# A decoder layer's output projection by Strassen's seven block products, in three phases with shared weight blocks

## The chip, the cores and the metric

The kernel runs on one core of one Trainium2 chip. The metric is the device time of one execution in microseconds (us), as the median of several runs; lower is better.

## What is computed

One layer of a decoder with an attention mixer, on 512 tokens of width 4096, in float32:

```
x: (1, 512, 4096)   64 query heads of 64, 8 key/value heads, window 128
h    = rms_norm(x, norm_g)
q, k, v, z = split(h @ w_in + b_in)          # w_in: 4096 x 9216
o    = banded attention with sinks (q, k, v) # (512, 4096)
x    = x + (o * silu(z)) @ w_out + b_out     # w_out: 4096 x 4096
out  = rms_norm(x, final_g)
```

The change is in the last two lines: the product with `w_out` and what follows it.

## The kernel before

All matmuls keep float32 accuracy by splitting each operand into a rounded part ("hi", float32r) and the rest ("lo"): ScalarE (ACT) casts hi (L143), VectorE (DVE) subtracts lo = source - hi (L144), and TensorE (PE) forms hi*hi + hi*lo + lo*hi, three matmuls of 128 columns of weights by 512 moving columns. All matmuls are issued by the helper `mm` (L112) and keep the order of the program on PE; on the other engines and queues a scheduler sets the order when the kernel is built.

The program has three stages. First V is projected and x is split (32 steps). Then 68 tiles of the input projection follow, each 8 chunks of 12 matmuls, with attention woven between the chunks (`at`, `tick`); `finish` (L510, L511) multiplies a head pair's output by its gate and writes it to a buffer `gT` in DRAM, from the POOL queue. During the last of these tiles `load_g` (L138) brings the gated outputs g back to SBUF, 512 tokens wide.

The third stage is the output projection, a loop over eight blocks of 512 output columns (`cc`), each over 32 K-tiles (`kt`) and four token blocks (`tb`):

```
for kt in kts:                               # mm_out
    if kt % 2 == 0: raw = load_w(w_out[cc, kt // 2])   # 512 KB on the SP queue, L170
    split_g(kt)                              # g split again for each cc
    w = split_w(raw, kt % 2)
    for tb, acc in enumerate(accs): mm_block(acc, tb, kt, *w)   # 3 matmuls each
```

That is 8 x 32 x 4 x 3 = 3072 matmuls. `bring` (L698 to L705) loads bias, gain and residual on POOL's queue and adds them on POOL, `land` (L711 to L714) adds the PSUM result and squares it, and after the last column block `scale_out` (L668 to L692) forms the norm and stores the rows. In the last column block the final ten K-tiles are held in SBUF (`held`), so that the token blocks end one after another. Tiles of x, g and their splits live in the pool `xg`, weights in `wpool`, attention's tiles in `att`, whose memory is free when attention has ended; the output's tiles (`outp`) are put there.

## Time and profile before

| | us |
|---|---|
| median of 3 runs (2407.26 to 2407.3) | 2407.3 |
| the profiled execution: its own time | 2406.92 |
| the profiled execution: span from first to last instruction | 2405.2 |
| output projection on PE, first to last matmul | 696.4 |
| PE busy, share of the span | 99% |
| DVE / ACT / POOL busy | 58% / 41% / 14% |

The sums of the prediction are made against the profiled execution, whose own time is 1.7 us over its span and 0.4 us under the median. An idle time on an engine that is not waited for costs nothing, so the question at each place is which wait ends last there. A granted clock of 1.00 is 2.4 GHz on TensorE, 0.50 is 1.2 GHz.

### The profile page before, as it was taken

To read this page: it belongs to the slowest core of one execution; us is meant where nothing else is said; L and a number is where in the kernel's file an instruction comes from. 1 tells how busy PE (TensorE), PEld (TensorE's weight loads), DVE (VectorE), ACT (ScalarE), POOL (GpSimd) and SP (SyncE) were. 2 spreads that over 40 slices of the span, in tenths; PEclk is the share of its full clock that TensorE was granted. 3 is DMA by queue.
4 is the path that set the end of the run, shared out by engine and by line. 5 is a ranking of instruction groups with operands and counts; after the bars stand their busy time and mean duration, and the time that the engine had idled before them with its cause. 6 is when DMAs were issued, how large, how long until landed. Compare 5 with 4: busy or idle time off the path is not lost.

```text
span 2405.2 us, 30234 instructions
## 1 busy us (share of the span) xinstructions
PE 2392.2 (99%) x10988; PEld 1991.1 (83%) x10988; DVE 1403.9 (58%) x2502; ACT 985.0 (41%) x2129; POOL 340.7 (14%) x472
## 2 busy tenths in 40 slices
PE   9999999999999999999999999999999999999998
PEld 7888888888888888888888888888888888888886
DVE  5446656555575564656656466565764664665565
ACT  6433433434343342433433334334444444444444
POOL 1101111121020121102102011111210110110110
PEclk9999999999999999999999999999999999999999
DMA  9633233233333323333233332334633433333334
GB/s 343 189 93 102 85 110 97 88 112 86 103 99 92 102 89 110 92 94 105 85 105 104 92 99 86 112 97 128 228 123 97 125 123 100 124 124 97 122 119 184
DMA packets 81077, 280.45 MB, mean 117 GB/s; under 512 B 10080, under 2 KB 10080, under 8 KB 80928
## 3 DMA queue, kind: packets, MB, share of 16 engines
q1 hardware_dynamic: 70176, 243.37, 32.7%
q0 software_dynamic: 10608, 34.88, 4.4%
q8 instruction: 86, 1.41, 0.2%
q14 instruction: 63, 0.52, 0.1%
q10 hardware_dynamic: 144, 0.28, 0.0%
HBM read 259.61 MB, written 18.88 MB: 116 GB/s over the span
## 4 chain that ended last, share of the span: by engine, by line
PE 99%; DMA 0%; DVE 0%; POOL 0%; ACT 0%; DVEq 0%; issue 0%; POOLq 0%
PE acc L112 94%; PE ps L112 2%; PE po L112 2%; PE pt L115 1%; DMA xraw<-in_x 0%; POOL wl L425 0%; POOL wh L425 0%; DVE y L688 0%; ACT xhi L241 0%; ACT y L712 0%; DVE xb L711 0%; DVEq L794 0%; DVE y L692 0%; POOL ww L425 0%; DVE y L678 0%
## 5 line engine op out<-in xcount | busy, mean ns | idle before, releaser
L144 DVE TENSOR_TENSOR wlo<-raw,whi 128x512 fp32r<-128x512 f32 x822 | 587.4, 716 | 760.2 <-ACT whi L143 751.5
L143 ACT CAST whi<-raw 128x512 fp32r<-128x512 f32 x821 | 510.7, 622 | 1204.1 <-PE acc L112 1148.3
L112 PE MATMUL acc<-xhi,wlo 128*128 128x512 f32 x2176 | 849.2, 390 | 0.0
L112 PE MATMUL acc<-xhi,whi 128*128 128x512 f32 x2176 | 848.6, 390 | 0.0
L112 PE MATMUL acc<-xlo,whi 128*128 128x512 f32 x2176 | 848.3, 390 | 0.0
L112 PE MATMUL acc<-whi,gs 128*128 128x512 f32 x1968 | 606.0, 389 | 0.0
L112 PEld LDWEIGHTS acc<-xhi,wlo 128*128 128x128 f32 x2176 | 408.4, 188 | 85.8
L112 PEld LDWEIGHTS acc<-xhi,whi 128*128 128x128 f32 x2176 | 409.1, 188 | 81.1
L112 PEld LDWEIGHTS acc<-xlo,whi 128*128 128x128 f32 x2176 | 408.4, 188 | 81.4
L112 PEld LDWEIGHTS acc<-whi,gs 128*128 128x128 f32 x1968 | 369.4, 188 | 76.7
L112 PE MATMUL acc<-wlo,gs 128*128 128x512 f32 x984 | 382.8, 389 | 0.0
L112 PEld LDWEIGHTS acc<-wlo,gs 128*128 128x128 f32 x984 | 184.7, 188 | 38.4
L144 DVE TENSOR_TENSOR gs<-g,gs 128x512 fp32r<-128x512 f32 x256 | 186.8, 770 | 0.7 <-ACT gs L143 0.7
L425 POOL TENSOR_SCALAR_AFFINE_SELECT ww<-wh 64x512 fp32r<-64x512 f32 x64 | 41.7, 651 | 881.7 <-ACT wh L421 881.7
L143 ACT CAST gs<-g 128x512 fp32r<-128x512 f32 x256 | 145.7, 616 | 1.7 <-PE acc L112 1.7
L497 DVE RECIPROCAL e<-e 128x128 f32<-128x128 f32 x128 | 120.6, 944 | 0.5
L399 ACT ACTIVATE prob<-ps,nm 128x128 f32<-128x128 f32 x256 | 90.4, 364 | 74.2 <-DVE nm L390 73.0
L704 POOL DMA_DIRECT2D xb<-in_x x32 | 17.3, 541 | 504.6 <-DVE y L714 430.8
L474 ACT COPY ot<-po 64x256 f32<-64x256 f32 x128 | 46.9, 367 | 56.8 <-DVE o L475 41.2
L475 DVE TENSOR_TENSOR o<-po,ot 64x256 f32<-64x256 f32 x128 | 52.8, 412 | 20.4 <-ACT ot L474 19.8
L348 DVE SCALAR_TENSOR_TENSOR q<-tmp,bcol,q 64x512 fp32r<-64x512 f32 x64 | 58.6, 916 | 7.2 <-ACT q L347 6.2
L274 DVE TENSOR_TENSOR tmp<-acc,rbc 128x512 f32<-128x512 f32 x37 | 25.6, 691 | 57.6 <-PE acc L112 57.6
(125 smaller groups left out, 1629.3 us busy)
## 6 DMA issues: line engine op xcount, KB each, us to landing
raw<-in_w_in SPq DMA_DIRECT2D x272, 512.0 KB, 3.6
raw<-in_w_out SPq DMA_DIRECT2D x128, 512.0 KB, 3.6
row<-in_x POOLq DMA_DIRECT2D x16, 512.0 KB, 6.5
gT<-o POOLq DMA_DIRECT2D x32, 256.0 KB, 2.3
g<-gT SPq DMA_DIRECT2D x16, 512.0 KB, 6.3
xb<-in_x POOLq DMA_DIRECT2D x32, 256.0 KB, 3.6
xraw<-in_xT SPq DMA_DIRECT2D x15, 512.0 KB, 7.1
raw<-in_w_v SPq DMA_DIRECT2D x15, 512.0 KB, 6.4
```

The source lines that it names most:

```text
L112: tc.keep_in_program_order(nc.tensor.matmul(*a, **k))
L115: tc.keep_in_program_order(nc.tensor.transpose(*a, **k))
L143: copy(hi, src),
L144: nc.vector.tensor_tensor(lo, src, hi.bitcast(F32), op=ALU.subtract),
L274: nc.vector.tensor_tensor(t, acc, rbc, op=ALU.mult)
L348: nc.vector.scalar_tensor_tensor(q2[other, :, h, :], tv[own], b[own], q2[own, :, h, :].bitcast(F32), op0=ALU.add, op1=ALU.subtract,)
L399: nc.scalar.activation(pr[:, u, a, :], ps[:, u, a, 0:P], AF.Exp, bias=nm[:, u, a:a + 1], scale=SCALE, accum_out=den[:, u, a:a + 1],)
L425: nc.gpsimd.affine_select(out=out, in_=src.bitcast(F32), fill=0.0, pattern=[[0, 8], [1 if own else -1, QH]], compare_op=ALU.is_ge if own e ...
L474: nc.scalar.copy(ot[own], pq[other, :, :, h, :])
L475: nc.vector.tensor_tensor(ov[own], pq[own, :, :, h, :], ot[own], op=ALU.add)
L497: nc.vector.reciprocal(c, c)
L704: nc.gpsimd.dma_start(xb, x[tb * P:(tb + 1) * P, cs])
```

## The change

The product (512 x 4096) @ (4096 x 4096) is taken as a 2 x 2 block product: G in halves of 256 tokens by 2048 of K (A11, A12, A21, A22), `w_out` in halves of 2048 of K by 2048 of columns (B11 to B22). It is formed by seven products instead of eight:

```
M1 = (A11+A22)(B11+B22)   M2 = (A21+A22) B11     M3 = A11 (B12-B22)
M4 = A22 (B21-B11)        M5 = (A11+A12) B22     M6 = (A21-A11)(B11+B12)
M7 = (A12-A22)(B21+B22)
C11 = M1+M4-M5+M7   C12 = M3+M5   C21 = M2+M4   C22 = M1-M2+M3+M6
```

They run in three phases, each over four column chunks `p` of 512 and eight weight steps `j`: `chunk_35` (M3 and M5, 24 matmuls and 2 weight loads a step), `chunk_167` (36 matmuls, 4 loads and one adding load a step) and `chunk_42` (24 matmuls, 2 loads). A step's weight tile is 128 x 1024. DVE forms the sums of blocks, except B21+B22, which is formed by a DMA that POOL issues and that adds onto the tile loaded before. The left operands are formed once (`left_35`, `left_167`, `left_42`) and kept in 16 numbered slots, which before held x's splits. Results accumulate in `y`, which starts as x plus bias: a load, and an adding DMA of the broadcast bias.

```diff
+def block_of(u, v, j):
+    kt = (v * NQ + j) * KC
+    return gT[kt:kt + KC, :, u * HALF:(u + 1) * HALF].rearrange("k p s -> p k s")
+def left(n, src):
+    t = slot(n, [P, 2, KC, HALF], "left")
+    split(src, t[:, 0], t[:, 1])
+    return t
+def stage_35(j):
+    staged[j] = slot(j % 2, [P, 2, KC, HALF], "stage", F32)
+    fetch_blocks(staged[j], (0, 0, j), (0, 1, j))
+def left_35(j):
+    t = staged[j]
+    a = left(L_35[j][0], t[:, 0])
+    nc.vector.tensor_tensor(t[:, 0], t[:, 0], t[:, 1], op=ALU.add)
+    L35[j] = a, left(L_35[j][1], t[:, 0])
+RING = (6, 7, 12, 13)
+FIRST = {
+    0: lambda: behind(lambda: (stage_35(0), stage_35(1))),
+    2: lambda: behind(lambda: left_35(0)),
+    3: lambda: behind(lambda: left_35(1)),
+    4: lambda: behind(lambda: stage_35(2)),
+    5: lambda: behind(lambda: left_35(2)),
+}
...
-                if t == NT - 1 and kc:
-                    behind(lambda: load_g(kc - 1))
+                if t == NT - 1 and kc in FIRST:
+                    FIRST[kc]()
...
+def raw_w(u, v, p, j):
+    pool = (wpool, outp)[take("raw") // RAW % 2]
+    raw = pool.tile([P, 2, CW], F32, name="raw", tag="raw", bufs=RAW)
+    nc.sync.dma_start(raw, part_w(u, v, p, j))
+    return raw
+def right(raw, place=None):
+    t = slot(RING[take("w") % 4] if place is None else place, [P, 2, 2, CW], "right")
+    split(raw, t[:, 0], t[:, 1])
+    return t
+def with_residual(t, tb, c0, w):
+    nc.sync.dma_start(t, x[tb * P:(tb + 1) * P, c0:c0 + w])
+    nc.gpsimd.dma_start(t, b_out[:, c0:c0 + w].broadcast_to([P, w]), accum_op=ALU.add)
+def chunk_35(p, between=()):
+    m3, m5 = accumulators(2)
+    for j in range(NP):
+        r12, r22 = raw_w(0, 1, p, j), raw_w(1, 1, p, j)
+        add(r12, r12, r22, ALU.subtract)
+        w3, w5 = right(r12), right(r22)
+        if j in between:
+            between[j]()
...
+        mm_pair(m3, j, L35[j // 2][0], w3)
+        mm_pair(m5, j, L35[j // 2][1], w5)
+        if j % 2 and p == NCC // 2 - 1:
+            left_167(j // 2)
...
+def chunk_167(p):
+    m1, m6, m7 = accumulators(3)
+    for j in range(NP):
+        r11, r22, r12, r21 = (raw_w(u, v, p, j) for u, v in ((0, 0), (1, 1), (0, 1), (1, 0)))
+        nc.gpsimd.dma_start(r21, part_w(1, 1, p, j), accum_op=ALU.add)
+        add(r22, r22, r11)
+        w1 = right(r22)
+        add(r12, r12, r11)
+        w6, w7 = right(r12), right(r21)
+        for m, l, w in zip((m1, m6, m7), L167[j // 2], (w1, w6, w7)):
+            mm_pair(m, j, l, w)
+        if j % 2 and p == NCC // 2 - 1:
+            left_42(j // 2)
...
+def chunk_42(p):
+    for j in range(NP):
+        r21, r11 = raw_w(1, 0, p, j), raw_w(0, 0, p, j)
+        add(r21, r21, r11, ALU.subtract)
+        w4 = right(r21)
+        late = last and j >= LATE
+        w2 = right(r11, (S_42[0] + S_42[1])[j - LATE] if late else None)
+        mm_pair(m4, j, L42[j // 2][0], w4)
+        if late:
+            held[j] = w2
+        else:
+            mm_pair(m2, j, L42[j // 2][1], w2)
...
+def begin():
+    for i in range(2):
+        for tb, h in ((2 + i, 1), (i, 0)):
+            y[tb, h] = outp.tile([P, D // 2], F32, name=f"y{tb}{h}", tag="y", bufs=4)
+            with_residual(y[tb, h], tb, h * (D // 2), D // 2)
...
+    chunk_35(p, () if p else {1: lambda: (stage_35(3), left_35(3)), 4: begin})
```

`begin` so sets up four half rows of y, 1 MB each, in the first chunk; `begin_21` does the same for the other four in the last chunk of the second phase, two of them read back from DRAM.

The queue of SP (loads) where the input projection ends: `raw` from `in_w_in` is the last tile's weights, `g` and `stage` are gated outputs, `raw` from `in_w_out` the first weights of the output projection. Before:

```order
L170 DMA raw_14357<-in_w_in 128x1024
L170 DMA raw_14476<-in_w_out 128x1024
L138 DMA g0_14192<-gT_89 128x2x512 x2
L138 DMA g1_14226<-gT_89 128x2x512 x2
L170 DMA raw_14515<-in_w_out 128x1024
```

With the change, from the load of B22 for step 1 (`raw_14494`), the first tile that lies in attention's memory, to that of B12 for step 4 (`raw_14607`):

```order
L668 DMA raw_14494<-in_w_out 128x1024
L189 DMA stage_14503<-gT_89 128x4x256
L668 DMA raw_14537<-in_w_out 128x1024
L668 DMA raw_14539<-in_w_out 128x1024
L700 DMA y21_14618<-in_x 128x2048
L700 DMA y00_14621<-in_x 128x2048
L700 DMA y31_14624<-in_x 128x2048
L700 DMA y10_14627<-in_x 128x2048
...
L668 DMA raw_14609<-in_w_out 128x1024
L755 DMA stage_15468<-gT_89 128x4x256
L755 DMA stage_15469<-gT_89 128x4x256
L668 DMA raw_14607<-in_w_out 128x1024
```

The weights of the output projection were alone with g; now the four 1 MB residual loads and three stage loads stand between those of steps 2 and 4, and the load of step 1 follows the end of attention.

DVE at the same place: the last tile's gate and product (`e`, `o`), whose write to `gT` ends attention. Before:

```order
L492 TENSOR_SCALAR e_14400<-e_14400 128x512
L497 RECIPROCAL e_14400<-e_14400 128x128 x2
L475 TENSOR_TENSOR o_14089<-po_14405,ot_14415 64x2x2x64
L497 RECIPROCAL e_14400<-e_14400 128x128 x2
L144 TENSOR_TENSOR wlo_14560<-raw_14554,whi_14559 128x512
L510 TENSOR_TENSOR o_14089<-o_14089,z_14152 128x512
L144 TENSOR_TENSOR wlo_14578<-raw_14554,whi_14577 128x512
L144 TENSOR_TENSOR gs_14634<-g2_14285,gs_14634 128x512
L500 SCALAR_TENSOR_TENSOR tmp_14398<-tmp_14398,bcol_84,e_14400 128x512
```

With the change:

```order
L549 TENSOR_TENSOR o_14089<-o_14089,z_14152 128x512
L539 SCALAR_TENSOR_TENSOR tmp_14407<-tmp_14407,bcol_84,e_14409 128x512
L549 TENSOR_TENSOR o_14089<-o_14089,tmp_14407 128x512
L681 TENSOR_TENSOR raw_14492<-raw_14492,raw_14494 128x1024
L147 TENSOR_TENSOR right_14500<-raw_14494,right_14500 128x1024
L202 TENSOR_TENSOR stage_14503<-stage_14503 128x1024
L147 TENSOR_TENSOR right_14497<-raw_14492,right_14497 128x1024
```

The splits that stood between the last products are gone, and DVE's next work is step 1's own.

DVE in the middle of `chunk_167`, with r11 `raw_16413`, r22 `raw_16415`, r12 `raw_16417`, r21 `raw_16419` of one step:

```order
L681 TENSOR_TENSOR raw_16417<-raw_16417,raw_16413 128x1024
...
L147 TENSOR_TENSOR right_16423<-raw_16415,right_16423 128x1024
L681 TENSOR_TENSOR raw_16473<-raw_16473,raw_16469 128x1024
L147 TENSOR_TENSOR right_16427<-raw_16417,right_16427 128x1024
L681 TENSOR_TENSOR raw_16471<-raw_16471,raw_16469 128x1024
L147 TENSOR_TENSOR right_16430<-raw_16419,right_16430 128x1024
L147 TENSOR_TENSOR right_16479<-raw_16471,right_16479 128x1024
```

The split of the tile that the DMA sums (`right_16430`) stands ahead of the next step's first split (`right_16479`), where before only splits of loaded tiles followed each other.

## Rows read from the trace of the kernel before

**Rows 1.** The page: busy time and share of the span, times instructions.
```profile
PE 2392.2 (99%) x10988; PEld 1991.1 (83%) x10988; DVE 1403.9 (58%) x2502; ACT 985.0 (41%) x2129; POOL 340.7 (14%) x472
```
**Rows 2.** Chain that ended last, in order of time: start, us, what.
```profile
1696.91 0.86 PE po L112 x5
1697.77 696.38 PE acc L112 x3072
2394.15 0.03 issue
...
2398.76 0.66 DVE y L692
```
**Rows 3.** Groups: line, shapes, count | busy, mean ns | idle before, releaser.
```profile
L112 PE MATMUL acc<-whi,gs 128*128 128x512 f32 x1968 | 606.0, 389 | 0.0
L144 DVE TENSOR_TENSOR wlo<-raw,whi 128x512 fp32r<-128x512 f32 x822 | 587.4, 716 | 760.2 <-ACT whi L143 751.5
L143 ACT CAST whi<-raw 128x512 fp32r<-128x512 f32 x821 | 510.7, 622 | 1204.1 <-PE acc L112 1148.3
L475 DVE TENSOR_TENSOR o<-po,ot 64x256 f32<-64x256 f32 x128 | 52.8, 412 | 20.4 <-ACT ot L474 19.8
```
**Rows 4.** Stretches: us, busy by engine, granted clock, DMA share, GB/s.
```profile
0.00:60.00 60.00, 58.43 (x251) 46.34 (x252) 33.24 (x53) 39.62 (x67) 7.91 (x22) 1.00 0.93 344
2000.00:2200.00 200.00, 200.00 (x884) 165.59 (x883) 113.93 (x163) 89.40 (x164) 20.96 (x20) 1.00 0.37 113
```
**Rows 5.** Groups by shape, as rows 3: ACT to 120 us; DVE, whole run.
```profile
L253 ACT ACTIVATE row<-row 128x1024 f32<-128x1024 f32 x16 | 16.9, 1056 | 7.9 <-DMA row<-in_x 7.8
...
L711 DVE TENSOR_TENSOR xb<-acc,xb 128x512 f32<-128x512 f32 x32 | 21.4, 686 | 15.3 <-PE acc L112 14.0 <-issue 1.3
```
**Rows 6.** DVE at the end of attention: start, us, line, shapes.
```profile
1697.32 0.68 DVE L274 TENSOR_TENSOR tmp<-acc,rbc 128x512 f32<-128x512 f32 x1
1697.92 0.68 DVE L144 TENSOR_TENSOR wlo<-raw,whi 128x512 fp32r<-128x512 f32 x1
1698.52 1.28 DVE L144 TENSOR_TENSOR gs<-g,gs 128x512 fp32r<-128x512 f32 x2
1699.73 0.41 DVE L475 TENSOR_TENSOR o<-po,ot 64x256 f32<-64x256 f32 x1
...
1708.05 0.69 DVE L144 TENSOR_TENSOR wlo<-raw,whi 128x512 fp32r<-128x512 f32 x1
1708.65 0.69 DVE L510 TENSOR_TENSOR o<-o,tmp 128x512 f32<-128x512 f32 x1
```
**Rows 7.** SP's queue there: the load behind the last `gT` write.
```profile
1712.28 0.38 SPq L138 DMA_DIRECT2D g<-gT  x1
```
**Rows 8.** DMA issues: engine, count, KB each, median us to landing.
```profile
raw<-in_w_out SPq DMA_DIRECT2D x128, 512.0 KB, 3.6
row<-in_x POOLq DMA_DIRECT2D x16, 512.0 KB, 6.5
gT<-o POOLq DMA_DIRECT2D x32, 256.0 KB, 2.3
...
raw<-in_w_v SPq DMA_DIRECT2D x15, 512.0 KB, 6.4
```
**Rows 9.** Stretches as in rows 4, behind the last matmul.
```profile
2396.00:2397.00 1.00, 0.00 (x0) 0.00 (x0) 0.85 (x4) 0.02 (x1) 0.00 (x0) 0.97 0.71 274
2397.00:2398.00 1.00, 0.00 (x0) 0.00 (x0) 0.96 (x3) 0.66 (x2) 0.00 (x0) 0.50 0.00 0
```
**Rows 10.** The same in 5 us stretches of the start.
```profile
5.00:10.00 5.00, 4.73 (x21) 3.49 (x19) 3.03 (x6) 2.68 (x5) 0.88 (x2) 1.00 1.01 399
10.00:15.00 5.00, 5.00 (x24) 4.13 (x23) 5.00 (x8) 4.03 (x7) 0.54 (x1) 1.00 1.03 404
...
20.00:25.00 5.00, 5.00 (x24) 4.14 (x23) 2.76 (x4) 3.18 (x7) 0.47 (x1) 1.00 1.03 406
```

More of the change, by code (lines that the diff above doesn't have):

```diff
@@ L641, in hybrid_block_kernel, with take, accumulators @@
-    for tb in (2, 3):
-        for t in ys[tb]:
-            nc.gpsimd.memset(t[:, 0:1], 0.0)
+    yd = dram.tile([2, P, D // 2], F32, name="yd")
+    count = {"raw": 0, "acc": 0, "w": 0}
+    def take(name):
+        count[name] += 1
+        return count[name] - 1
+    def accumulators(n):
+        return [
+            [((ps_m, ps_n)[take("acc") // 4 % 2]).tile([P, CW], F32, name="acc") for _ in range(2)]
+            for _ in range(n)
+        ]
+    def raw_w(u, v, p, j):
[3 more added lines that the diff above has]
+        return raw
@@ new lines, in part_w, with add, mm_block @@
+    def part_w(u, v, p, j):
+        return w_out[NCC // 2 * v + p, NP * u + j].rearrange("p (j c) -> p j c", j=2)
+    def right(raw, place=None):
+        t = slot(RING[take("w") % 4] if place is None else place, [P, 2, 2, CW], "right")
+        split(raw, t[:, 0], t[:, 1])
+        return t
+    def add(out, a, b, op=ALU.add):
+        nc.vector.tensor_tensor(out, a, b, op=op)
+    def mm_block(acc, i, j, lt, rt):
+        for m in range(2):
+            l = lt[:, :, (2 * j + m) % KC, i * P:(i + 1) * P]
+            mm(acc, l[:, 0], rt[:, 0, m], start=(j == m == 0), stop=False)
+            mm(acc, l[:, 0], rt[:, 1, m], start=False, stop=False)
+            mm(acc, l[:, 1], rt[:, 0, m], start=False, stop=(j == NP - 1 and m == 1))
@@ new lines, in hybrid_block_kernel, with left_167 @@
+    L167 = {}
+    S_167 = ((14, 15, 0), (1, 2, 3), (4, 5, 8), (9, 10, 11))
+    def left_167(j):
+        t = [outp.tile([P, KC, HALF], F32, name="stage", tag="stage", bufs=3) for _ in range(3)]
+        for b, k in zip(t, ((0, 0), (1, 1), (1, 0))):
+            nc.sync.dma_start(b, block_of(*k, j))
+        a11, a22, a21 = t
+        a, b, c = S_167[j]
+        add(a21, a21, a11, ALU.subtract)
+        l6 = left(b, a21)
+        add(a11, a11, a22)
+        l1 = left(a, a11)
+        a12 = outp.tile([P, KC, HALF], F32, name="stage", tag="stage", bufs=3)
+        nc.sync.dma_start(a12, block_of(0, 1, j))
+        add(a12, a12, a22, ALU.subtract)
+        L167[j] = l1, l6, left(c, a12)
@@ L666, in scale_out @@
         )
-        last = sq[tb][:, NCC - 1:NCC]
+        *more, cc = sorted(fresh)
+        last = sq[tb][:, cc:cc + 1]
+        for c in more:
+            nc.vector.scalar_tensor_tensor(
+                part, sq[tb][:, c:c + 1], 1.0 / D, part, op0=ALU.mult, op1=ALU.add
+            )
         nc.scalar.activation(a, last, AF.Sqrt, bias=part, scale=1.0 / D)
```

231 lines of the change are left out of this document (131 added, 100 removed).

## The prediction

> **What bounds the kernel now.** The page's first section comes first: PE is busy for 99% of the span, DVE 58%, ACT 41% [rows 1]. The chain that ended last, in order of time, confirms it for the stage that changes: one piece on PE, from 1697.77 us for 696.38 us, holds all 3072 matmuls of the output projection without another engine in it, and 11 us of norm and stores follow the last one [rows 2]. So a matmul there costs 696.38 / 3072 = 0.2267 us; the mean of 389 ns in the groups [rows 3] is a latency, since matmuls overlap. DVE and ACT wait, for PE and for each other [rows 3], and in the middle of the stage the DMA engines are busy 37% of the time at 113 GB/s [rows 4]. PE's work is the bound, and everything beside it has room: until the change fills it.
>
> **What is removed.** Seven products of 4 x 8 x 12 = 384 matmuls take the place of eight: 2688 for 3072, of the same shape (128 weight columns, 512 moving). 384 x 0.2267 = **87.0 us** off the path, and 609.4 us of matmuls stay. The repeated splitting of g (256 pairs of an ACT and a DVE instruction) and POOL's residual adds go too; they were beside PE and are worth nothing.
>
> **DVE and ACT.** Tiles are now 1024 wide. A DVE tensor_tensor took 686 ns at 512 columns [rows 5] and 412 ns at 256 [rows 3], 1.07 ns a column, so 686 + 512 x 1.07 = 1.24 us; ACT took 1.06 us at 1024 [rows 5]. A step of the first and last phase asks DVE for one sum and two residues, 3.7 us beside 24 matmuls = 5.44 us; a step of the middle phase for two and three, 6.2 us beside 36 matmuls = 8.16 us. Both fit. Left operands add 7.4 us to DVE for a pair of steps in the phase before they are needed, spread by free slots. In the last chunk, steps 4 to 7 hold M2 back, so 12 matmuls (2.7 us) face 3.7 us of DVE: at most 4 us, less the lead. With a second square before the last norm I take **4 us** (0 to 8) for these ends.
>
> **Seam 1: the second step waits for attention.** SP loads B22 of step 1 into attention's old memory, so it follows the last write to gT, and DVE's difference, ACT's cast and DVE's residues follow the load. Before, g's tail had 30 K-tiles of work in front of it and nobody waited. When did that write land? The last gate product ended at 1708.65 + 0.69 = 1709.3 [rows 6], and SP, which waited for the write, went on at 1712.3 [rows 7]. Between the last tile's evacuation at 1697.3 and that product stood eight splits, each some 0.6 us apart (of these the first three and the last are shown [rows 6]); the new order has none there. So the write lands about 8 x 0.6 = 4.8 us sooner, at 1707.5. The load adds 3.6 us [rows 8]: 1711.1. Then difference 1.24 and cast 1.06 let the first matmul go, and since one other residue and a sum stand in front on DVE, its own residue ends 4 x 1.24 = 5.0 us after the load, 1716.1. PE has step 0 until then, 1697.8 + 5.4 = 1703.2. PE idles for **12.5 us** (8 if the order were kinder, 17 if the tail is as before).
>
> The clock: 2.8 us after the last matmul the granted clock went from 1.00 to 0.50, that is from 2.4 to 1.2 GHz [rows 9], so PE comes back at the slow level. No row shows it rise again. A matmul at half clock costs up to 0.23 us more; between nothing and a step of 24 (5.4 us) for each long wait I take **4 us** for two (0 to 11).
>
> **Seam 2: residual loads in front of weights.** Behind step 2's weights SP has issued four loads of 1.05 MB, two of 0.26 MB, three of 0.52 MB for left operands and the two weight tiles of step 4: 7.3 MB. The fullest stretches of the start moved 399 to 406 GB/s [rows 10], so this takes 18.3 us. Step 2's weights land at about 1715, step 4's then at 1733.5, ready at 1736. PE has steps 1 to 3, 1716 + 3 x 5.44 = 1732.3: a wait of 4 us if these loads were alone. But POOL's adding DMAs for the bias (4.7 MB) start as each y lands and run on the same engines. If all of them went ahead they would add 12 us at the price of a plain transfer and 24 us at twice that. **15 us** (4 to 28), about half of the dearer one.
>
> **What an adding DMA costs** is in no row. From below: a plain transfer of 512 KB, 1.31 us at 400 GB/s. From above: the 6.5 us that a POOL load took to land at the crowded start [rows 8], as if the engines did nothing else, five transfers. It must read the tile from SBUF, as the writes to gT do, besides the weights from DRAM, so I take two transfers, 2.6 us. The Trainium skill ("Collectives: The Full Stack", section "The bandwidth ceiling: the fold count and why AG ≠ RS ≠ AR") says that a DMA which adds emits two read descriptors on one read ring and halved the rate there (32 against 62 GB/s); by that page the price is the same two transfers, and the sum below would not move. No run so far shows it.
>
> **The middle phase.** A step moves four loads and one adding DMA: 6 x 1.31 = 7.86 us beside 8.16 us of PE. The order adds a loop: the summed tile's buffer is free after the residue of the previous step's first tile; then load, add, cast and residue follow, and the next step's first residue stands behind on DVE. Two steps (16.3 us) hold 1.06 + 2 x 1.24 = 3.5 us of these and leave 12.8 us for load and add together. Loads landed in 3.6 us when little ran and 6.4 in the crowd [rows 8]; the add by POOL is 6.5 us in the crowd and 1.3 us more for the second read. 10.1 to 14.2 us: about even. I take 8.4 us a step, 32 x 0.25 = **8 us** (0 to 30). In its last chunk 7.9 MB for the third phase come on top (five left blocks, two read-back and one residual half row, one bias add at two transfers): 19.6 us, less the 0.3 us of room in eight steps, and some of it can lie over the chunk's end: **14 us** (4 to 22).
>
> **The sum.** 87.0 - 12.5 - 4 - 15 - 8 - 14 - 4 = 29.5 us. Span 2405.2 - 29.5 = 2375.7, with the 1.7 us around the span 2377.4, with 0.4 us from this execution to the median **2378 us**, 1.2% faster. Its own range, with the bounds not all at once on one side, is 2355 to 2402.
>
> **Rival 1: the add costs a plain transfer.** Then a middle step moves 6.6 us of data, load and add fit the loop, the phase waits nowhere, its last chunk loses 4 us and seam 2 about 8: 87.0 - 12.5 - 3 - 8 - 4 - 4 = 55.5 us, **2352 us**. For it: the two operands come from different memories. Against: both go through the same DMA engine. Chance 0.20.
>
> **Rival 2, on the other side: the adding DMA becomes the bound of the middle phase.** At five transfers a step moves 9 x 1.31 = 11.8 us, 3.6 over PE, 116 us in 32 steps: more than all that was saved. At three it moves 9.2 us, 33 us over, with seam 2 at 24 and the last chunk at 20: 87.0 - 12.5 - 4 - 24 - 33 - 20 - 4 = -10, 2418 us. It decides from about 2.9 transfers on, where the gain is gone. At three and a half (9.8 us, 53 us over; the other terms as at three) it gives **2438 us**. For it: such an add has never run here, and its latency is in series with a load in a loop that has no slack. Chance 0.18.
>
> **Rival 3: 400 GB/s does not last.** The 400 GB/s are 5 us stretches; over the first 60 us it was 344 GB/s at a share of 0.93 [rows 4]. At that rate 3.15 MB a step take 9.15 us, 32 us over, the last chunk 22, seam 2 20: 87.0 - 12.5 - 4 - 20 - 32 - 22 - 4 = -7.5, **2415 us**. Against: the share was below one, so demand and not the engines may have set the 344. The Trainium skill ("DMA: Bandwidth & Descriptors", Specifications) gives about 358 GB/s as what HBM yields to one core. By that page a step would take 8.8 us and the result would be some 2396 us. The trace disagrees in short stretches, 406 GB/s [rows 10], and for these the measurement decides; a long one is not shown. Chance 0.10.
>
> That the change does not do what it says is unlikely: the new PE order holds the 2688 matmuls in the same shape. Chance 0.02 that their pace differs.
>
> **How the numbers follow.** Forecast 0.50, rivals 0.20, 0.18, 0.10, the rest 0.02. A measurement here tells about 0.2% (4.8 us) from no change, so faster is below 2402.5. The forecast's range lies below that almost whole (0.46 of 0.50), rival 1 all of it, rival 3 by 0.02, the rest 0.01: faster 0.69. Same 0.06, from the upper edge of the forecast and the lower of rivals 2 and 3; slower 0.25. The range leaves out rival 1's lower half (0.10, under 2350) and rival 2's upper part (0.10, over 2445): **2350 to 2445**.
>
> **What would show it.** The first phase: PE idle near 1703 for 10 to 15 us, released by DVE's residue behind SP's load of B22, the clock at 0.50 after it; a second wait at step 4, and an issue-to-landing time of the 1 MB adding DMAs far over that of the loads. The middle phase: matmuls from 8.2 to 8.9 us a step, DMA share near one in it, at 320 GB/s or more, and the last chunk longer than the three before. 2688 matmuls at 0.2267 us in the rest. The adding DMA's landing time decides between the forecast and rivals 1 and 2: about 3.5 us alone means one transfer, 5 us two, 8 us or more rival 2. I am wrong above all if DVE's order, not data, makes PE wait in the middle phase (it is 76% busy there and cast, residue and sum are in series), or if the seams overlap differently: an earlier load of step 1 would give 12.5 us back.

## The result, and the profile of the changed kernel

The changed kernel takes **2562.4 us**, the kernel before 2407.3 in the same comparison: a ratio of 1.0647, with an interval of 1.0628 to 1.0665. It is 6.5% slower; the forecast was 2378 us and the range ended at 2445. The profiled execution spans 2557.9 us, 152.7 more than that of before (2405.2).

From the page of the changed kernel, as in [rows 1, 3, 8]: shares of the engines; the software DMA queue, POOL's (packets, MB, share of 16 engines); groups (busy us, mean ns, idle before); DMA issues (median us to landing).

```profile
PE 2395.6 (94%) x10604; PEld 1945.4 (76%) x10604; DVE 1541.1 (60%) x2462; ACT 950.7 (37%) x1867; POOL 313.0 (12%) x454
...
q0 software_dynamic: 14992, 52.70, 8.6%
...
L115 PE MATMUL acc<-xhi,whi 128*128 128x512 f32 x2176 | 863.3, 397 | 0.0
...
L115 PE MATMUL acc<-right,left 128*128 128x512 f32 x2688 | 663.4, 406 | 133.2 <-ACT right L146 67.6
...
raw<-in_w_out SPq DMA_DIRECT2D x256, 512.0 KB, 5.5
...
raw<-in_w_out POOLq DMA_DIRECT2D x32, 512.0 KB, 8.7
```

PE has fallen from 99% to 94% and now waits 133 us for weights. But the first matmul row, of the input projection, is unexpected too: 397 ns, in code that the diff does not touch, where the page of before has 390:

```profile
L112 PE MATMUL acc<-xhi,whi 128*128 128x512 f32 x2176 | 848.6, 390 | 0.0
```

The same by stage (busy us of each engine, granted clock, DMA share, GB/s). The stretches are the end of the input projection and the three phases; a phase is taken to begin when ACT has cast its first weights.

```profile
1690.00:1743.00 53.00, 42.69 (x184) 34.79 (x183) 39.00 (x69) 23.74 (x55) 11.24 (x14) 0.84 0.43 138
...
1743.00:1978.00 235.00, 180.18 (x756) 142.98 (x755) 154.85 (x156) 80.35 (x88) 17.66 (x25) 0.91 0.76 240
1978.00:2330.00 352.00, 294.55 (x1162) 226.68 (x1160) 229.87 (x217) 108.79 (x112) 30.07 (x36) 0.94 0.88 268
2330.00:2541.00 211.00, 189.51 (x780) 151.50 (x780) 151.46 (x185) 86.13 (x117) 4.14 (x7) 0.94 0.58 183
```

The matmuls of the phases need 174.1, 261.2 and 174.1 us at 0.2267 us each. They took 234, 351 and 211. PE is idle in a part of the difference (57 us in the middle phase); in the rest it is called busy. A part of that is the granted clock, 0.91 to 0.94 here: behind 21 of the 70 waits of over 0.3 us the matmuls start 0.43 us apart instead of 0.227, at the lower of the two levels (0.50 from 2028.8 to 2031.0 us, for one).

| where the time went | predicted | measured |
|---|---|---|
| 384 matmuls fewer | -87.0 | -87.0 |
| output projection starts later (1697.77 to 1743.87) | 0 | +46.1 |
| seam 1, wait at the second step | +12.5 | +13.3 |
| seam 2, wait at step 4 of the first chunk | +15 | +28.2 |
| rest of the first phase (234.2 - 174.1 - 41.5) | 0 | +18.6 |
| middle phase (351.4 - 261.2) | +22 | +90.2 |
| third phase (211.0 - 174.1) | +4 | +36.9 |
| after the last matmul (17.5, before 11.1) | in the 4 | +6.4 |
| clock | +4 | in the rows above |
| sum | -29.5 | +152.7 |

ACT casts ahead of PE, and not by the same lead everywhere. Counted from the first matmul of each phase on PE instead, the three last 238.8, 361.2 and 196.5 us: by that count some 14 us of the third phase's row belong to the middle one, and 5 of the middle one's to the first.

### The profile page after: what moved, and what is told of

Same layout as the page of the kernel before. It is cut to its first block, busy times and chain, and to the rows that moved or that the text cites. A ratio compares the mean times of both kernels' runs of the same rounds, so it can differ in the third digit from the quotient of the medians.

```text
span 2557.9 us, 29388 instructions
## 1 busy us (share of the span) xinstructions
PE 2395.6 (94%) x10604; PEld 1945.4 (76%) x10604; DVE 1541.1 (60%) x2462; ACT 950.7 (37%) x1867; POOL 313.0 (12%) x454
## 4 chain that ended last, share of the span: by engine, by line
PE 70%; DMA 16%; DVE 9%; issue 4%; ACT 1%; SPq 0%; POOL 0%; DVEq 0%; ACTq 0%; POOLq 0%
PE acc L115 65%; DMA raw<-in_w_out 13%; DVE right L147 3%; DMA stage<-gT 2%; DVE raw L681 2%; PE ps L115 2%; PE po L115 2%; DVE y L681 1%; PE pt L118 1%; DMA y<-in_x 1%; ACT right L146 0%; DVE left L147 0%; DMA yd<-st 0%; DVE stage L681 0%; DVE st L681 0%
## 5 line engine op out<-in xcount | busy, mean ns | idle before, releaser
L115 PE MATMUL acc<-xhi,whi 128*128 128x512 f32 x2176 | 863.3, 397 | 0.0
L115 PE MATMUL acc<-right,left 128*128 128x512 f32 x2688 | 663.4, 406 | 133.2 <-ACT right L146 67.6
L115 PEld LDWEIGHTS acc<-right,left 128*128 128x128 f32 x2688 | 520.5, 196 | 275.8 <-DVE right L147 87.6
L147 DVE TENSOR_TENSOR wlo<-raw,whi 128x512 fp32r<-128x512 f32 x576 | 402.9, 700 | 527.6 <-ACT whi L146 518.3
L146 ACT CAST whi<-raw 128x512 fp32r<-128x512 f32 x575 | 357.0, 621 | 880.6 <-PE acc L115 833.9
L146 ACT CAST right<-raw 128x1024 fp32r<-128x1024 f32 x224 | 230.1, 1047 | 435.9 <-DMA raw<-in_w_out 223.0
L147 DVE TENSOR_TENSOR right<-raw,right 128x1024 fp32r<-128x1024 f32 x224 | 268.4, 1218 | 71.9 <-ACT right L146 71.5
L681 DVE TENSOR_TENSOR raw<-raw 128x1024 f32<-128x1024 f32 x128 | 156.2, 1222 | 176.8 <-DMA raw<-in_w_out 169.0
L771 POOL DMA_DIRECT2D raw<-in_w_out x32 | 27.5, 859 | 318.8 <-DVE raw L681 172.1
L447 DVE TENSOR_SCALAR prob<-prob,den 128x128 f32<-128x128 f32 x256 | 56.0, 282 | 2.2
```

What stands on the lines that cost most here:

```text
L115: tc.keep_in_program_order(nc.tensor.matmul(*a, **k))
L146: copy(hi, src),
L147: nc.vector.tensor_tensor(lo, src, hi.bitcast(F32), op=ALU.subtract),
L447: nc.vector.tensor_scalar_mul(pr[:, u, a, :], pr[:, u, a, :], den[:, u, a:a + 1])
L681: nc.vector.tensor_tensor(out, a, b, op=op)
L771: nc.gpsimd.dma_start(r21, part_w(1, 1, p, j), accum_op=ALU.add)
```

## The experiments

Eighteen kernels ran, each once, c3 four times (its stages are those of one execution, of 2485.4 us). The four runs of the changed kernel lie between 2559.7 and 2567.0 us. Each kernel starts from the changed kernel unless it says otherwise; times are to be compared with 2562.4 us. Stages in us: when the output projection's first matmul starts, then the three phases. Where a run left the middle phase alone it still took 342 to 359 us, so less than some 10 us in one run is not read as an effect.

| run | time | start | first | middle | third |
|---|---|---|---|---|---|
| changed kernel | 2562.4 | 1743.9 | 234.2 | 351.4 | 211.0 |
| a_pad | 2516.5 | 1710.1 | 234.3 | 342.3 | 210.5 |
| a_noadd | 2498.7 | 1742.5 | 235.6 | 293.4 | 208.2 |
| a_plain | 2522.3 | 1741.8 | 236.9 | 312.9 | 211.3 |
| a_dvesum | 2521.6 | 1744.2 | 236.1 | 315.0 | 208.0 |
| a_deep | 2550.3 | 1743.3 | 240.8 | 335.0 | 211.6 |
| a_deepdve | 2517.5 | 1742.9 | 237.5 | 308.5 | 209.6 |
| a_deepmix | 2531.6 | 1744.5 | 235.5 | 329.3 | 203.4 |
| a_yq | 2547.5 | 1743.9 | 228.3 | 346.6 | 209.5 |
| a_nobias | 2526.1 | 1743.1 | 205.7 | 352.2 | 206.0 |
| a_late | 2519.0 | 1742.9 | 200.4 | 346.1 | 210.8 |
| a_seam1 | 2550.9 | 1742.8 | 227.2 | 358.8 | 203.1 |
| a_tail | 2537.5 | 1740.5 | 227.8 | 349.9 | 199.7 |
| c1 | 2474.0 | 1709.6 | 216.7 | 318.2 | 210.3 |
| c2 | 2500.2 | 1711.1 | 216.2 | 340.8 | 212.8 |
| c3 | 2490.6 | 1710.5 | 203.5 | 357.9 | 194.3 |
| c4 | 2452.5 | 1704.8 | 198.9 | 333.8 | 196.1 |
| c5 | 2440.7 | 1704.8 | 200.5 | 316.2 | 200.0 |

### Why the untouched input projection became slower

The chain of waits (start us, us, what) of before shows 49.00 us for 216 matmuls of the input projection, that of the changed kernel 50.40. The diff moves the pool of `whi` and `wlo`: their offset in SBUF goes from 30848 bytes, a multiple of 128, to 177728, 64 bytes past one.

**a_pad**: the same instructions in the same order, 64 bytes further on.

```
+    small.tile([P, 16], F32, name="pad")     # att, and whi and wlo in it, start 64 bytes later
```

> The changed kernel with 64 unused bytes ahead of the pool that now holds whi and wlo: these start on a multiple of 128 bytes again (offset 177792 instead of 177728), all instructions and their order stay. In the changed kernel the input projection, which the diff does not touch, ran at 0.2333 us a matmul (50.40 us for 216) against 0.2267 before, and its last matmul ended at 1743 us against 1696. Theory A (address): the place of whi and wlo is the cause; the pace returns to 0.2267, the last matmul of the input projection ends some 37 us sooner and the time falls from 2562 to about 2525 us. Rival B (something else of the new layout, such as xhi and xlo lying in turns, or whi and wlo sharing a pool with attention): the pace stays at 0.2333 and the time at 2562 us.

**b_shift**: the kernel before, with the reverse.

```
     def split_w(raw, j, copy=nc.scalar.copy):
+        if latest[1] is None: wpool.tile([P, 16], F32, name="pad1")
         hi = wpool.tile([P, CW], F32R, name="whi", tag="whi", bufs=WB)
         lo = wpool.tile([P, CW], F32R, name="wlo", tag="wlo", bufs=WB)
+        if latest[1] is None: wpool.tile([P, 16], F32, name="pad")
```

> The kernel before with 64 unused bytes ahead of whi and wlo and 64 behind them: only these two lie 64 bytes off a multiple of 128, everything else stays on one, and the order of all instructions is the same. Theory A (address): the input projection slows to 0.2333 us a matmul as in the changed kernel, some 37 us, and if a moving operand off the multiple costs the same, the output projection (whi and wlo are the moving operand there) goes from 696 to some 715 us as well: 2445 to 2465 us in all. Rival B (another part of the layout): 2407 us, 0.2267 in both.

The chain of before has

```profile
209.66 49.00 PE acc L112 x216
```

that of the changed kernel

```profile
213.54 50.40 PE acc L115 x216
```

that of a_pad

```profile
209.80 48.99 PE acc L115 x216
```

and that of b_shift

```profile
214.03 50.40 PE acc L112 x216
...
1729.66 716.04 PE acc L112 x3072
```

a_pad took 2516.5 us, 45.9 less, and the output projection starts 33.8 us sooner; the other 12 lie behind it, 9 of them in the middle phase, and are not more than that phase varies by. a_pad also moves attention's tiles and some weight buffers by 64 bytes; in b_shift whi and wlo alone leave a multiple of 128. b_shift took 2459.7, 52.3 more than before. In these stretches 64 bytes alone move a matmul between 0.2267 and 0.2333 us, in both directions, whether whi and wlo are the stationary operand (input projection) or the moving one (output projection, 716.04 us for 696.38 [rows 2]). Theory A holds. Of the 46.1 us, 33.8 are the address. The other 12 stand in the last input tile, in PE's timeline:

```profile
1719.95 0.58 PE L115 MATMUL po<-wh,vv 128*128 128x256 f32 x1 [2.64 <-POOL wh L464]
...
1734.52 1.08 PE L118 MATMUL pt<-ident,prob 128*128 128x128 f32 x4 [7.64 <-DVE prob L447]
```

The new left operands stand ahead of attention's last work (`prob`) in DVE's order:

```profile
1730.49 1.23 DVE L147 TENSOR_TENSOR left<-stage,left 128x1024 fp32r<-128x1024 f32 x1 [2.77 <-ACT left L146]
...
1734.09 0.87 DVE L447 TENSOR_SCALAR prob<-prob,den 128x128 f32<-128x128 f32 x4
```

With one of them moved behind the tile, in c5, the longer wait was 3.0 us. The prediction had given DVE's order at this place no cost.

### What the adding DMA costs in the middle phase

**a_noadd** drops its line (M7's weights are then B21 alone), **a_plain** drops only the adding (B22 alone), **a_dvesum** sums on DVE and leaves nothing out.

```
-            nc.gpsimd.dma_start(r21, part_w(1, 1, p, j), accum_op=ALU.add)
+            nc.gpsimd.dma_start(r21, part_w(1, 1, p, j))        # a_plain
+            add(r21, r21, r22)                                  # a_dvesum
             add(r22, r22, r11)
```

> The changed kernel without the adding DMA of the middle phase: the seventh product's weights are B21 alone, so 32 adding DMAs and the value of B22 in them are left out. In the changed kernel a step of the middle phase took 10.8 us against 8.16 us of matmuls. Theory A (the adding DMA is the cause, by its place in the loop of load, add, cast and residue over six buffers): the step falls to 8.2 to 8.6 us and the time by 70 to 85 us, to some 2480 us. Rival B (DVE's own order is the cause, sums and residues in series with the loads): the step stays over 10 us and the time over 2540 us.

> The changed kernel with the 32 adding DMAs of the middle phase made plain: the same transfer from the same queue at the same place with the same waits, but it overwrites, so the seventh product's weights are B22 alone. It separates what adding costs from what a second, later transfer costs. Theory A (the loop's latency sets the step): the add goes from two transfers to one, 1.3 us less in a loop of two steps, 0.6 us a step, 20 us in all, 2540 us. Rival B (the DMA engines' throughput sets it): a step moves five transfers, 6.4 us, under PE's 8.16; the step falls to 8.2 to 8.6 us and the time to some 2480 us, as without the add. The software queue's share of the 16 engines (8.6% for 52.7 MB) falls by 1.6 points if adding costs twice a plain transfer.

> The changed kernel with B21 + B22 summed by DVE ahead of the sum that overwrites B22, which is in a buffer anyway: no adding DMA in the middle phase and nothing left out. DVE then has three sums and three residues a step, 6 x 1.22 = 7.3 us of 8.16. Theory A (the adding DMA was the cost): as without the add, 2495 to 2505 us. Rival B (DVE at 90% is the next bound, above all at the ends of chunks where it also adds up the products): half of it is given back, 2515 to 2535 us.

First the price. The pages of a_plain and of a_noadd, to be held against the q0 line of the changed kernel above:

```profile
q0 software_dynamic: 14992, 52.70, 6.9%
...
q0 software_dynamic: 10384, 35.92, 5.0%
```

The same packets and bytes take 8.6% of 2557.9 us with adding and 6.9% of 2520.6 without: 46 us of 16 engines in 32 DMAs, 1.4 us more each. Without these 32 DMAs it is 5.0% of 2497.0 us, so a plain one costs 1.5 us and an adding one 3.0: about **two transfers**, as predicted. The Trainium skill ("Collectives: The Full Stack", section "The bandwidth ceiling: the fold count and why AG ≠ RS ≠ AR") has two read descriptors for the add of a ReduceScatter, and the rows agree with it. Rival 2 decided from 2.9 transfers on, and for three it had 33 us; the phase lost 90. The price alone was not what decided.

The chain in the middle phase of the changed kernel shows what did:

```profile
2103.44 7.72 DMA raw<-in_w_out
2111.24 0.06 DVE raw L681
2111.31 1.08 issue
2112.39 1.23 DVE right L147
2113.63 8.74 DMA raw<-in_w_out
```

and so on every 10.8 us. A residue frees a weight buffer, SP's load into it takes about 8.3 us to land, DVE's sum waits for it, and the next residue stands behind that sum in DVE's order and frees the next buffer only then. The adding DMA is not itself on this chain, but the plain loads beside it land later: the median from issue to landing, between 1980 and 2300 us, is 6.8 us in the changed kernel and 4.9 in a_noadd.

```profile
raw<-in_w_out SPq DMA_DIRECT2D x117, 512.0 KB, 6.8
...
raw<-in_w_out SPq DMA_DIRECT2D x136, 512.0 KB, 4.9
```

In a_noadd the DMA pieces of the chain are some 5 us long:

```profile
2074.23 5.01 DMA raw<-in_w_out
2079.37 1.23 DVE raw L681
...
2084.03 5.51 DMA raw<-in_w_out
```

The middle phase fell to 293 us without the add and to 313 with a plain transfer in its place. Of the 90 us over, 58 hang on the add: some 38 on the adding and 20 on having a fifth transfer at all. The time of a_noadd fell by 64 us, a little short of its Theory A (70 to 85). Neither expectation of a_plain was met: the gain of 40 us lies between 20 (latency alone) and 80 (throughput alone). With DVE's sum the phase fell by 36 us instead of 58, as Rival B of a_dvesum had it; DVE is then busy for 265 of 315 us.

**a_deep**: nine buffers instead of six, in three of the four chunks.

```
+    n = take("deep") // RAW % 3
+    raw = (wpool, outp, outp)[n].tile([P, 2, CW], F32, tag=("raw", "raw", "stage")[n], bufs=RAW)
```

> The changed kernel with nine weight buffers instead of six in the first three of the four chunks of the middle phase (the three stage buffers, idle there, join the ring); the adding DMA stays as it is. A step took 10.8 us, without the adding DMA 9.2, with a plain one 9.8. Theory A (latency in a ring of 1.5 steps: a weight tile is loaded only when the one 1.5 steps earlier is used up, and load, add, cast and residue follow in series): with 2.25 steps of ring the steps of these chunks fall to 8.3 to 8.9 us and the time by 45 to 60 us, to some 2510 us. Rival B (throughput of DMA engines or DVE): the step stays over 10 us and the time over 2545 us.

**a_deepdve** and **a_deepmix** have nine buffers from the seventh step on, with all or half of the sums on DVE.

> The changed kernel with nine weight buffers from the seventh step of the middle phase to the end of its third chunk, and DVE's sum instead of the adding DMA. With nine buffers and the adding DMA the fifth and sixth of the twelve chunks still took 10.1 us a step, the DMA share at 0.91; with six buffers and DVE's sum 9.5 us, the share at 0.68. Theory A (two limits: the ring's latency with few buffers, the DMA engines' throughput with many, since an adding packet takes twice the time): without adding packets and with the deep ring the step falls to 8.2 to 8.7 us and the time to some 2495 us. Rival B (DVE, at 7.3 us a step and the sums of chunks on top): the step stays at 9.3 us or more, 2515 us or more.

> As the nine buffers with DVE's sum, but only every other step's sum is DVE's, the rest adding DMAs: 6.7 us of DVE and 6.4 us of the DMA engines a step, neither near 8.16. Theory A: 8.2 to 8.6 us a step, 2490 to 2500 us. If DVE alone had been the limit with its sums, this is 10 us or more faster than that kernel; if the adding DMA's latency still sets the step where it stands, it is 10 us or more slower.

The second and third of the four middle chunks, 16 steps, by windows (length first; granted clock and DMA share are the two columns before the last). The changed kernel:

```profile
2072.00:2243.00 171.00, 147.84 (x578) 113.98 (x577) 104.07 (x97) 48.29 (x50) 13.59 (x16) 0.93 0.82 242
```

a_plain:

```profile
2063.00:2212.00 149.00, 138.03 (x588) 111.18 (x587) 102.92 (x97) 48.94 (x49) 8.46 (x16) 0.98 0.80 279
```

a_noadd:

```profile
2047.00:2195.00 148.00, 135.50 (x584) 108.34 (x583) 101.61 (x97) 50.27 (x49) 0.00 (x0) 1.00 0.69 226
```

a_dvesum:

```profile
2064.00:2215.00 151.00, 138.69 (x578) 110.19 (x577) 122.97 (x112) 48.73 (x49) 0.00 (x0) 0.97 0.68 223
```

a_deep:

```profile
2072.00:2234.00 162.00, 145.05 (x607) 113.68 (x608) 106.87 (x102) 49.93 (x49) 13.76 (x17) 0.99 0.91 270
```

a_deepdve:

```profile
2062.00:2204.00 142.00, 134.73 (x579) 107.39 (x578) 120.21 (x113) 50.35 (x49) 0.00 (x0) 1.00 0.71 235
```

a_deepmix:

```profile
2071.00:2214.00 143.00, 133.34 (x569) 105.35 (x568) 109.16 (x103) 48.91 (x48) 6.83 (x8) 1.00 0.84 261
```

These stretches run from cast to cast. Counted from the first matmul of one chunk on PE to that of the next, a step of the four chunks took (us; PE needs 8.16):

| run | 1 | 2 | 3 | 4 |
|---|---|---|---|---|
| changed kernel | 11.6 | 10.6 | 10.8 | 12.2 |
| a_plain | 10.7 | 8.8 | 9.5 | 11.2 |
| a_noadd | 8.9 | 9.0 | 9.3 | 9.3 |
| a_dvesum | 10.3 | 9.5 | 9.4 | 10.7 |
| a_deep | 11.9 | 10.0 | 9.4 | 11.9 |
| a_deepdve | 10.3 | 8.9 | 8.8 | 10.6 |
| a_deepmix | 11.1 | 9.3 | 9.1 | 11.2 |

In the second and third chunk the deep ring alone brings 1 us a step, with the DMA engines busy for 91% of the stretch (its 2550.3 us are Rival B's); the adding taken away alone brings 1.2 to 1.5; both together (a_deepdve) come within 0.7 us of PE. a_deepdve is no slower there than a_deepmix, so DVE's load is not the limit of these two chunks. In the first and the last chunk left operands come on top, and the ring has six buffers for most of the first and all of the last; there each DVE sum costs 1.4 us a step (a_dvesum against a_noadd), and half of the adds more still (a_deepmix). a_deepmix, expected at 2490 to 2500 us, was 14 us slower than a_deepdve; its text had put such a result down to the adding DMA's latency, which no run tested in these two chunks alone.

The windows also give the DMA engines' work in a step, busy share times length by 16: 8.8 us as changed, 6.4 in a_noadd. A plain load of 512 KB thus took 1.6 us of the engines, where the prediction had 1.31, and a step with the adding DMA asks for more than PE's 8.16.

### Seam 2 and seam 1

PE in the timeline of the changed kernel:

```profile
1743.87 5.65 PE L115 MATMUL acc<-right,left 128*128 128x512 f32 x24
1761.15 0.80 PE L115 MATMUL acc<-right,left 128*128 128x512 f32 x1 [11.64 <-ACT right L146]
1763.59 18.16 PE L115 MATMUL acc<-right,left 128*128 128x512 f32 x71 [1.65 <-DVE right L147]
1808.43 0.80 PE L115 MATMUL acc<-right,left 128*128 128x512 f32 x1 [26.69 <-ACT right L146]
1810.71 18.48 PE L115 MATMUL acc<-right,left 128*128 128x512 f32 x71 [1.48 <-DVE right L147]
```

and SP in the same stretch:

```profile
1756.35 2.29 SPq L700 DMA_DIRECT2D y<-in_x  x4
...
1766.74 23.77 SPq L755 DMA_DIRECT2D stage<-gT  x2
1790.62 17.02 SPq L668 DMA_DIRECT2D raw<-in_w_out  x6
```

SP issued the residual loads and left operands, then stood for 24 us (21.3 of them in the second of these two issues alone), and the weights of step 4 behind them went out from 1790.6. The profile names nothing that the long issue waited for.

**a_nobias**: without the adding DMAs of the bias, which is then missing in the output. (Its text counts twelve; there are fourteen, eight of 256 KB and six of 1 MB.)

> The changed kernel without its twelve adding DMAs of the bias (eight of 256 KB, six of 1 MB are meant together: all that add b_out to the residual rows); the bias is left out of the output, the plain residual loads stay where they are. The prediction put PE's wait at step 4 of the first chunk at 4 us if the plain loads were alone and took 15 us with the adds; 26.7 us were measured. If the plain loads alone cost 4 us, the wait falls to 2 to 7 us and the time by 20 to 30 us, to some 2537 us. Rival (SP's queue: the weights wait for the landings of the 1 MB loads ahead of them, whatever adds beside them): the wait stays over 15 us and the time over 2550 us.

**a_yq** brings the residual by quarters; **a_late** also ties each quarter, the other residual loads, and the middle phase's left operands, behind the weights of its own step.

```
+        between = {4: lambda: begin(p)}                     # a_yq: columns p * CW only
+        between = {4: lambda: behind(lambda: begin(p))}     # a_late
-                left_167(j // 2)
+                behind(lambda: left_167(j // 2))            # a_late
```

> The changed kernel with the residual rows and bias brought in by quarters: at step 4 of each of the four chunks of the first phase only the 512 columns that this chunk needs (four loads and four adding DMAs of 256 KB), instead of all 2048 columns (four of 1 MB) in the first chunk. The bytes stay the same. In the changed kernel PE waited 26.7 us once at step 4 of the first chunk, at the lower clock after it. Theory A (a burst ahead of the weights in SP's order): the wait falls below 6 us, the later chunks have room for their quarter, and the time falls by 22 to 32 us, to some 2535 us. Rival B (the data has to come anyway): four waits of some 6 us take the place of one, 2555 to 2565 us.

> The changed kernel with the transfers of the first seam held back in SP's order: residual rows by quarters, each issued only behind the weights of step 4 of its own chunk (with quarters alone, all sixteen loads were issued in the first chunk all the same, and the time fell by 15 us), and the loads for the middle phase's left operands only behind the weights of the last chunk's steps (before: three of them ahead of the weights of step 4 of the first chunk). Theory A (a burst ahead of the weights in SP's order): PE's wait of 26.7 us at step 4 falls below 4 us, and with the clock that follows it the time falls by 25 to 35 us, to some 2532 us. Rival B (bytes and adding DMAs set it wherever they stand): the waits of the first phase stay over 40 us in all and the time over 2550 us.

PE's timeline at seam 2 in a_nobias:

```profile
1785.76 0.80 PE L115 MATMUL acc<-right,left 128*128 128x512 f32 x1 [4.75 <-ACT right L146]
1789.16 32.31 PE L115 MATMUL acc<-right,left 128*128 128x512 f32 x132 [2.61 <-DVE right L147]
```

SP at the same issue there:

```profile
1768.81 3.23 SPq L754 DMA_DIRECT2D stage<-gT  x1
```

and PE around both seams in a_late:

```profile
1759.56 0.80 PE L115 MATMUL acc<-right,left 128*128 128x512 f32 x1 [11.04 <-ACT right L146]
1763.03 48.12 PE L115 MATMUL acc<-right,left 128*128 128x512 f32 x204 [2.67 <-DVE right L147]
```

Without the bias adds the wait is 7.4 us (4.75 + 2.61) for 28.2: the plain loads alone cost 7, the adds 21. SP's long issue took 3.2 us for 21.3; why the adds hold it up was not settled. With the same bytes in another order there is no wait at this place: in a_late 204 matmuls run without a stop, and the time falls by 43 us, of which 34 lie in the first phase. The order let the wait arise, and the adding DMAs made it large. a_yq missed (15 us): the scheduler issued all sixteen quarters in the first chunk, since nothing held them.

**a_seam1** puts four early weight buffers into x slots that are free.

```
+        if RAW <= n < RAW + 4:                  # tiles 4 to 7 of the first phase
+            raw = early[0][:, (n - RAW) % 2]    # halves of slots 14 and 15
```

> The changed kernel with four weight buffers of the first phase's second and third step in the two x slots that the input projection's last matmuls free, so that they do not lie in attention's memory. In the changed kernel PE waited 11.6 us and then 1.7 us at the second step. Theory A (memory of attention, as predicted): 8 to 13 us less, some 2551 us. Rival B (the next load in SP's queue that reads gT, for the last left operand, stands ahead of the third step's weights, and the wait only moves there): less than 4 us, over 2558 us.

In its timeline PE waits 2.75, 3.59 and 1.37 us at the second to fourth steps, 7.7 us for 13.3; the first phase is 7 us shorter. (The time fell by 11.6 us, as Theory A had it, but the other 4 lie in phases that the edit does not touch.) The memory was the cause of about half; the rest is waits for the casts and residues behind it, in part what Rival B had.

### The chunks' ends

In the third phase of the changed kernel, DVE's timeline at a chunk's end:

```profile
2388.91 2.48 DVE L681 TENSOR_TENSOR y<-acc,y 128x512 f32<-128x512 f32 x4
...
2392.43 0.68 DVE L681 TENSOR_TENSOR y<-acc,y 128x512 f32<-128x512 f32 x1
2393.03 0.67 DVE L681 TENSOR_TENSOR y<-y,acc 128x512 f32<-128x512 f32 x1
2393.63 0.68 DVE L681 TENSOR_TENSOR y<-y,fg 128x512 f32<-128x512 f32 x1
```

Fourteen such sums and scalings, some 9 us of DVE, stand here among the next steps' weights, where a step leaves DVE 1.7 us.

**a_tail** splits them into pairs and issues one or two pairs behind each step of the next chunk.

```
+            behind(lambda: pay(2))       # third phase; pay(1) in the first
```

> The changed kernel with the sums at a chunk's end spread in the first and the third phase: instead of 10 to 14 DVE instructions in a row at the border, one or two pairs stand behind each step of the next chunk. Nothing else moves. The third phase took 210 us for 174 us of matmuls and loses some 5 us at each border and more behind it. Theory A (DVE, busy with a chunk's sums for 7 to 9 us, lets the weights of the next steps come late): the third phase falls by 15 to 25 us, the first by 5 to 15, the time to some 2530 us. Rival B (DVE has the same work in the end, or the loads are what is late): less than 8 us, over 2554 us.

2537.5 us, 25 less: the third phase fell by 11 us and the first by 6, the start by 3; the rest is inside what the middle phase varies by. The cause is Theory A's, at the lower end of its price in the first phase and under it in the third (15 to 25 expected): it accounts for about a third of the 55 us that these two phases lost beside the seams. What the other two thirds are was not settled.

### All edits together

**c1** to **c5** add edits up. c1 is a_pad, a_dvesum, a_yq and a_seam1, c2 the same with the sum on POOL.

> Four edits at once: the 64 bytes that put whi and wlo back on a multiple of 128, DVE's sum in place of the adding DMA in the middle phase, residual rows by quarters, and four weight buffers of the first phase's second and third step in the x slots that the input projection frees, so that they wait for no attention memory. Nothing is left out. If the gains add: 2562 - 46 (measured for the first) - 55 - 27 - 12 = 2422 us. If the waits are one chain in which each edit only uncovers the next one: above 2445 us.

> As the kernel with the four edits, but POOL adds B22 to B21 instead of DVE. If DVE's load is what is left in the middle phase, this is 10 to 25 us faster than with DVE's sum (POOL was busy 12% of the span); if POOL's sum is slow (over 4 us for 1024 columns) or stands in POOL's queue behind other work, it is no faster. Expected: 2405 to 2415 us.

c1 took 2474.0 us and c2 2500.2, so the gains did not add up, and POOL's sum was no help: it took 2.6 us for 1024 columns, and DVE's sums then waited 56 us in all for it. In c1's middle phase the DVE sum left 318 us.

c3 is a_pad, a_seam1, a_late, a_deep and a_tail, with the adding DMA.

> Five edits together, the adding DMA kept and nothing left out: 64 bytes ahead of the pool of whi and wlo (46 us measured), early weight buffers in freed x slots (13), residual and left operands held back (30), nine buffers in the middle phase (50), the chunks' sums spread (25). If the terms add, 2562 - 164 = 2398 us, 0.4% faster than the kernel before. If waits are only moved from one place to the next, half of the last three is lost: 2450 us.

c3 took 2490.6 us (1.0350 of before, 1.0333 to 1.0367). This is slower than either figure expected. The deep ring's first loads stood behind the last left operands: one wait of 33 us.

c4 takes these loads from the seventh step on, has the sums of a_deepmix and issues the residual's pieces sooner, and one left operand behind the last input tile; c5 is c4 with the sum of a_dvesum.

> All edits together, nothing left out: whi and wlo on a multiple of 128 (46 us measured), residual and left operands held back (43 measured), the chunks' sums spread, the residual's pieces early enough for them (25 measured), nine buffers from the seventh step of the middle phase with every other sum on DVE (60 expected), and the left operands of the input projection's end and the load of the last of them moved behind weights (10 to 15 expected). If the terms add, 2562 - 186 = 2376 us, 1.3% faster than before. In the earlier sum of edits they did not, because the deep ring's first loads stood behind left operands (33 us) and the residual's pieces came late; if more of that kind is left, 2410 to 2440 us.

> As the kernel with all edits, with every sum of the middle phase on DVE and no adding DMA there. If DVE's load is the limit of the middle phase by then, some 15 us slower than with every other sum on DVE; if the adding DMA's latency is, as much faster.

c4 took 2452.5 us, over its upper figure, and c5 2440.7, so by then the adding DMA cost more than DVE's sums. The windows of c5's phases:

```profile
1704.00:1905.00 201.00, 182.85 (x773) 146.11 (x773) 149.23 (x151) 78.91 (x87) 28.45 (x38) 0.97 0.86 273
1905.00:2221.00 316.00, 270.82 (x1117) 215.16 (x1117) 271.08 (x252) 113.83 (x114) 2.56 (x4) 0.94 0.75 251
2221.00:2422.00 201.00, 191.15 (x803) 151.09 (x803) 154.38 (x190) 86.91 (x119) 4.15 (x7) 0.98 0.62 193
```

122 of the 155 us are recovered, but no version here beats the kernel before. What is left, against the matmuls, is 26 us in the first phase, 26 in the third and 55 in the middle one, where DVE is busy for 271 of 316 us.

## Why the prediction was wrong, step by step

- **87 us of matmuls saved**: right: 2688 matmuls of the same shape, and most of them start 0.227 us after the one before.
- **The input projection, taken as unchanged** (the sum starts the output projection at 1697.8, as before): the step that failed first, and never written as a term (the chance of 0.02 was for the pace of the new matmuls). It cost 46 us: 34 by an address, 12 by DVE's order. These alone turn the predicted gain of 29 into a loss.
- **Seam 1**: right, 12.5 predicted and 13.3 measured. The load of B22 went out at 1754.3 us, behind the last write to gT, 10.4 us after the projection's first matmul (9.7 predicted). Left out of the account was what stands behind this wait: without it (a_seam1) 7.7 us remain.
- **Seam 2**: the mechanism was right and the size off. 28 us stand at the upper bound (4 to 28); the adds cost 21 us where half of the dearer 24 was taken, and SP's issue of 21 us was no part of it.
- **Price of the adding DMA**: right, two transfers. **Middle phase**: wrong, and the largest miss. The term compared 7.86 us of transfers a step with 8.16 us of PE; 8.8 were measured, since a plain load took the engines 1.6 us and not 1.31. It then weighed load plus add, 10.1 to 14.2 us, against 12.8 in two steps and called it even. Landings were 6.8 (loads) and 8.7 us (adds) in this phase, 15.5 together. And the loop on the chain was another one: every step waited for the landing of a plain load, with DVE's sum and residue in series. 90 us, four times the term; even the upper bounds (30 + 22) fell short. Only the extra of the last chunk was right: 12 us over the two chunks before it, counted on PE, where 14 were taken. The prediction's last sentence named DVE's order as what would make it wrong, but gave it no price.
- **Rival 2** (the adding DMA as the bound): its price of three transfers or more did not come, but a part of its reason did, a landing in series in a loop without slack. The sign that was to tell it, a landing of 8 us or more, came too (8.7), with the forecast's price of two transfers: under this load the landing time did not tell the price.
- **Rival 3** (a lower lasting rate): its 9.15 us of transfers a step were nearer to the measured 8.8 than the forecast's 7.86, so 400 GB/s did not last here. Alone it does not explain a step of 10.7: a_plain moved more (279 GB/s for 242) and was faster.
- **First and third phase**: "both fit" was an average of DVE over a step. A chunk's end asks for 10 to 14 instructions more at once, and the term of 4 us counted only the last chunk.
- **Clock**: 4 us for two waits. With some 70 waits, PE's busy time exceeds the matmuls' by 6, 33 and 15 us in the three phases. In these, 16, 80 and 27 matmuls start 0.38 to 0.46 us apart instead of 0.227, at the lower clock: 3, 16 and 5 us, 24 us for the 4. In a_noadd, at 1.00, PE's busy time still exceeds that of its 584 matmuls by 3 us, so short gaps are a part of the rest.

## What to carry to other kernels

When a pool moves, compare the offsets of the operands of the matmuls before and after: 64 bytes cost 34 us here, more than the 29 that the whole change was to gain. A phase whose average demand on DVE and DMA fits under PE still fails if buffers are freed, loaded and used through one engine's order: follow one buffer around its loop, with landing times taken under the load of that phase, and count the extra work at each border. And see what stands ahead of the weights in a queue: the same bytes in another order were worth 34 us in the first phase.

## What the runs showed of the chip that was not expected

- A 128 x 128 by 512 matmul of these float32r operands takes 0.2333 us instead of 0.2267 (216 in 50.40 us instead of 49.00) when one of its operands lies 64 bytes past a multiple of 128 bytes in SBUF, stationary or moving (a_pad, b_shift); other offsets were not run. The Trainium skill ("SBUF — State Buffer", section "Operand start alignment") asks only for a multiple of the element size, and says that this is about legality, not speed. The runs add the speed.
- An adding DMA from DRAM into SBUF costs about twice a plain one in engine time (3.0 us for 1.5, 512 KB), and the loads beside it land later: a median of 6.8 us over most of the middle phase, 4.9 without it.
- One load's issue on SP lasted 21.3 us while large adding DMAs ran, and 3.2 us without them (a_nobias).
